# Moving the update of the sample states from the mixer to the gate and up tiles of the next stage

## Chip, cores, metric

One NeuronCore of a Trainium2 chip. The metric is the device time of one launch in microseconds (us), lower is better. A kernel is described by the median over its runs; one execution is profiled.

## What is computed

One inference step of a two-layer decoder trunk on 512 prompt rows and 8 sample rows (one new token for each of 8 sequences), all in fp32. Each layer has a SwiGLU FFN, a token mixer (a gated DeltaNet head group beside a sliding-window attention group) and a second SwiGLU FFN. Each of the three adds to the residual stream `x` through shift, scale and gate vectors ("modulation") that come from a conditioning vector. Cut to what the change touches, the DeltaNet step of a sample row, per head, with a state S of 128 x 128:

```python
# one token per sample row: the chunk has length 1
S      = S * jnp.exp(g)                     # decay
v_new  = beta * (v - k @ S)                 # what the state does not yet hold
o      = q @ S + (q . k) * v_new            # output, then gated RMSNorm
S_new  = S + outer(k, v_new)                # is an output of the function
```

The output `o` needs the old state and `v_new`, not `S_new`: the updated state is only stored (`new_dn_S_sample`, 8 sequences x 4 heads x 128 x 128 for each of 2 layers). Nothing later in the step reads it.

## The kernel before

Activations stand transposed, 128 features on the partitions and 512 + 8 columns, cut into a half of 256 and a half of 264. Matrix products are done in fp32 precision by splitting weights and activations into a high and a low part (`whi`/`wlo`, `hh`/`hl`): ScalarE rounds the high part, VectorE subtracts to get the low part, and TensorE does three products. Weight blocks arrive by DMA on SyncE's queue (SP) into four buffers (`raw`), and `Stream` splits them in pieces of 512 columns up to eight pieces ahead of their use.

Program order on every engine is fixed when the program is built. A planner (`Clock`, L40; `Fill`, L101) keeps modelled times of each engine, and during the long weight products it is asked at many points (`fill.step()`, L138) whether a piece of other work may be put in. Pieces are Python generators with a rank; the one of lowest rank that is ready by the model runs up to its next `yield`. A `yield` of tiles means "ready when those are written", of a function "ready when it returns true". `step` asks for a free PSUM bank, for ScalarE at most 2.4 us and VectorE at most 7.7 us behind TensorE in the model (L31, L145), and for nothing else.

An FFN (`ffn`, L849) has gate and up tiles f = 0 to 21 in two parts (0 to 10, 11 to 21), each part followed by a down projection. The first tiles (the `head`) are plain; from tile 3 a gate and up pair is done by `seven()` (L886) with seven block products where eight would be plain. It needs sums and differences of the weight blocks (`sum`, VectorE) and of the activations (`th`, made from `ht` by `combine`, L811, as the FFN starts), and its products of the two columns are put together by ScalarE (`u`) and VectorE (`g`, `u`). Its banks: `pa` and `pc` are the two halves of an `acc` buffer, `pb` an `aux` buffer into which five of the products accumulate with reads in between.

The mixer (`mix`, L1036) does the input projection, then attention and DeltaNet as filling work, then the output projection (`tail`, L770), whose tiles are added to `x` by VectorE (`xupdate`, L689). The sample part of DeltaNet is `dn_sample` (L1389), with `sample_pair` (L1417) for each pair of heads: it takes 7 slots (`hold(7)`), loads four state tiles `st` of 128 x 512 (four sequences of one head each), does the products with them, stores the rows of `v_new` to DRAM (`vnd`), loads them back spread over all partitions (`bv`), decays the states on GpSimd (L1486), adds the outer products on VectorE, four per state tile (L1496), and stores the tile (L1498). After that the second pair begins. In the trace the state tiles are called `s`, and the helper lines stand for all operations: L322 DMA, L328 matrix products, L338 transposes, L355 ScalarE, L363 VectorE, L374 and L376 GpSimd.

Most tiles share 51 slots of SBUF. `used` counts the named ones, `given` those taken by `hold` until they are given back; `given` is set to 0 as a mixer starts (L1039), and four that are held for the first output weights (`open_keep`, L1800) stay in the count until the next mixer. The modulation vectors are made by `ada_gen` (L515) at rank 9 from 18 groups per layer, each of eight loads (`ada`, 256 KB) and eight narrow products; a group is loaded when `fits()` (L525) finds room: 51 slots less `spares`, which is 13 during the gate and up tiles and 4 in the down projections (L982, L984). Layer 1's 18 groups are done in layer 0's second FFN.

Of the kernel before, what the change touches and what calls it, by code (L numbers as in the profile page):

```python
# [12 lines left out]
ALU = mybir.AluOpType  # L13
# [4 lines left out]
KD = D // 128  # L18
# [7 lines left out]
SLOTS = 51  # L26
# [276 lines left out]
class Ops:  # L303
# [68 lines left out]
    def pool(self, f, **k):  # L372
        if f == "memset":
            self.nc.gpsimd.memset(k["out"], k["value"])  # L374
        else:
            getattr(self.nc.gpsimd, f)(**k)  # L376
        self.clk.run("pool", 0.1 + 0.003 * self.cols(k["out"]), [k["out"]], self.aps(k, ("in_", "in0", "in1")))

    def tt(self, **k):
        self._dve("tensor_tensor", self.cols(k["out"]), k)  # L380

    def stt(self, **k):
        self._dve("scalar_tensor_tensor", self.cols(k["out"]), k)
# [22 lines left out]
def trunk(ctx, tc, xT, cT, cst, rope, vec, gu1, dn1, win, wba, wout, gu2, dn2, ada,  # L406
# [12 lines left out]
    mm, act, tt, stt, ts, dma, pool = ops.mm, ops.act, ops.tt, ops.stt, ops.ts, ops.dma, ops.pool  # L419
    fill = Fill(clk)  # L420

    used, given = set(), [0]
# [52 lines left out]
    def ada_load(l, g):  # L475

        t = []
        for k in range(KD):
            a = slot("ada", F32, (128, 512))
            dma(out=a, in_=ada[l, g, k])  # L480
            t.append(a)
        ada_live.extend(t)
        return t
# [26 lines left out]
    room = [True]  # L510

    spares = [13]
    mod_done = {(0, 0), (0, 1)}

    def ada_gen(l0):  # L515

        todo = []

        def more():
            if not todo and room[0] and mods and mods[0][0] <= l0:  # L520
                l, j = mods.pop(0)
                todo.extend((l, j, u) for u in range(2))
            return todo

        def fits():  # L525
            return len(used) + KD <= SLOTS - spares[0]

        queue, pa = [], None
        while True:
            while more() and len(queue) < 2 and fits():  # L530
                l, j, u = todo.pop(0)
                queue.append((l, j, u, ada_load(l, 2 * j + u)))
            if not queue:
                if not more():
                    return
                yield fits
                continue
            l, j, u, t = queue.pop(0)
            yield t
            if not u:  # L540
                pa = aux()
            ada_mm(t, pa, u)
            if u:
                m_sb = ada_out(pa)
                yield m_sb,
                ada_turn(l, 2 * j, m_sb, None, 2)
                drop(m_sb)
                mod_done.add((l, j))
            else:
                yield ()  # L550
# [298 lines left out]
    def ffn(l, j, norm, nxt, last, first=None, plain=3):  # L849
# [7 lines left out]
        def go(n=1):  # L857
            for _ in range(min(n, len(late))):
                late.pop(0)()
# [26 lines left out]
        def seven():  # L886

            pa, pb, pc = banks.pop(0) if banks else (None, aux(), None)  # L890
            if pa is None:
                u = acc()
                pa, pc = u[:, 0], u[:, 1]
            if pb is None:
                pb, pc = aux(), aux()
            t = slot("g")
            u1, u2 = (slot("u", F32, (128, 2, 264)) for _ in range(2))
            t0, t1 = t[:, 0:256], t[:, 256:520]

            def of_h(a, k0, n):  # L900
                return lambda _, part, k: hh[a][part][:, k0 + k, 0:n]

            def of_t(i, c, n=264):
                return lambda _, part, k: th[k][i + part][:, c, 0:n]

            def prod(bank, n, src, first):
                w = W.take()
                for k in range(4):
                    mmk(bank[:, 0:n], w, k, src, k, 0, first and k == 0, k == 3, join=not first)
                    W.advance(W.out - 1)  # L910
                    if k % 2:
                        fill.step()
                go()

            prod(pb, 264, of_h(0, 0, 264), True)
            act(out=u1[:, 0], in_=pb[:, 0:264], func=AF.Copy)
            prod(pa, 256, of_h(0, 4, 256), True)
            tt(out=t0, in0=pa[:, 0:256], in1=u1[:, 0, 0:256], op=ALU.add)
            prod(pb, 264, of_t(0, 1), False)
            act(out=u1[:, 1], in_=pb[:, 0:264], func=AF.Copy)  # L920
            act(out=t0, in_=t0, func=AF.Silu)
            prod(pc, 264, of_t(0, 0), True)
            act(out=u2[:, 1], in_=pc[:, 0:264], func=AF.Copy)
            prod(pb, 264, of_t(2, 0), False)
            tt(out=u2[:, 1], in0=pb[:, 0:264], in1=u2[:, 1], op=ALU.add)
            prod(pc, 264, of_h(1, 4, 264), False)
            tt(out=t1, in0=pc[:, 0:264], in1=u1[:, 1], op=ALU.add)
            prod(pb, 256, of_t(2, 1, 256), False)
            act(out=t1, in_=t1, func=AF.Silu)
            tt(out=t0, in0=t0, in1=pb[:, 0:256], op=ALU.mult)  # L930

            def end():
                tt(out=t1, in0=t1, in1=u2[:, 1], op=ALU.mult)
                drop(u1, u2)

            later(end, *split(t))
# [36 lines left out]
        for part, (f0, f1) in enumerate(PARTS):  # L973
            nk = f1 - f0
            for f in range(max(f0, 2), f1):
                if f < plain:
                    pg = product(h_src)
                    pu = product(h_src)
                    gate(pg, pu)
                    continue  # L980
                fill.until(lambda: len(th) == 4)
                spares[0] = 13  # L982
                seven()
            spares[0] = 4  # L984
            go(len(late))
            if part:
                room[0] = False
                for x_ in th:
                    drop(*x_)

            def g_src(a, p, k):
                o, n = HALF[a]
                return (ghi, glo)[p][f0 + k][:, o:o + n]

            fill.until(lambda: (l, 3 * j + 2) in mod_done)
            if part:
                if nxt:
                    ops.table(EXP)
                    n1 = (l, j + 1) if j < 2 else (l + 1, 0)
                    fill.until(lambda: {(n1[0], 3 * n1[1]), (n1[0], 3 * n1[1] + 1)} <= mod_done)  # L1000
                    nrm = nxt()
            for m in range(KD - 2 if part else KD):
                p = product(g_src, nk)
                for a in range(2):
                    xupdate(l, j, m, p[a], a)
                    if nrm is not None:
                        nrm.square(m, a)
                if part and last:
                    dma(out=y_o[:, m], in_=x[:, m])
            if part:  # L1010
                y, z = KD - 2, KD - 1
                items = [(0, y, True, True, True), (0, z, True, True, True), (1, y, False, False, True), (1, z, False, False, True)]
                tail(l, j, items, nk, nrm, g_src, last)
            drop(*ghi[f0:f1], *glo[f0:f1])
# [21 lines left out]
    def mix(l, norm):  # L1036
# [380 lines left out]
        def sample_pair(pr, qv, beg, d8, i8, bc, on):  # L1417

            hs = slice(2 * pr, 2 * pr + 2)
            st = [slot("s0", F32, (128, 4, 128), True) for _ in range(4)]  # L1420
# [54 lines left out]
            bv = []  # L1475

            def load(i):
                bv.append(slot("bv", F32, (128, 4, 128), True))
                o = 32 * (i // 2) + 4 * (i % 2)
                dma(out=bv[i], in_=rows[o:o + 4].partition_broadcast(128))  # L1480

            load(0)
            load(1)
            for i in range(4):
                h, s1 = 2 * pr + i // 2, 4 * (i % 2)
                pool("tensor_tensor", out=st[i], in0=st[i],  # L1486
                     in1=bc[:, h, s1:s1 + 4].unsqueeze(2).to_broadcast([128, 4, 128]), op=ALU.mult)
            yield vr,
            p = aux((128, 2, 32))
            ops.transpose(p.rearrange("p h s -> p (h s)"), vr[:, 2], cs[P, C_ID:C_ID + 64])  # L1490
            stt(out=on[:, hs], in0=p[:, :, 0:NS], scalar=V[:, V_DNW:V_DNW + 1], in1=zs[:, hs], op0=ALU.mult, op1=ALU.mult)
            for i in range(4):
                yield bv[i], st[i]
                h, s1 = 2 * pr + i // 2, 4 * (i % 2)
                for c in range(4):
                    stt(out=st[i][:, c], in0=bv[i][:, c], scalar=qv[:, h, 1, s1 + c:s1 + c + 1], in1=st[i][:, c],  # L1496
                        op0=ALU.mult, op1=ALU.add)
                dma(out=ss_o[l, :, 16 * pr + 4 * i:16 * pr + 4 * i + 4, :], in_=st[i])  # L1498
                if i < 2:
                    load(i + 2)  # L1500
            given[0] -= 7

        def out_sample(src, k0):
            hi, lo = hh[1]
# [575 lines left out]
```

## Time and profile before

| | |
|---|---|
| median of 3 runs | 2230.0 us (2226.77 to 2231.2) |
| the profiled execution | 2231.2 us, span 2229.4 us |
| mean granted TensorE clock | 0.984 of full speed |
| TensorE matmul / weight load busy | 96% / 90% |
| VectorE, ScalarE, GpSimd busy | 69%, 49%, 4% |
| HBM traffic | 287.76 MB, 129 GB/s |

Busy time is the time in which an engine works on an instruction; the span runs from the first instruction to the last. The stages of layer 0 lie at about 0 to 430 us (first FFN), 430 to 745 (mixer), 745 to 1180 (second FFN); those of layer 1 at 1180 to 1546, 1546 to 1845 and 1845 to 2229. In a timeline, a row gives the start, the time from the start of its first to the end of its last instruction, engine, line, operation, output and inputs, shapes, the count and in brackets the idle time of the engine before it with what ended it. Durations of neighbouring instructions overlap by some 0.08 us on VectorE and more on TensorE.

### The profile page before, as it was taken

The page shows a single profiled execution, that of the slowest core. Times are in us where ns is not written, and L with a number is a line of the kernel's source. Part 1 is how long each engine was busy: PE and PEld are TensorE (multiplying, and loading weights), DVE is VectorE, ACT ScalarE, POOL GpSimd, SP SyncE. Part 2 cuts the span into 40 slices and gives each one's busy share as a digit, 9 for nine tenths or more (in the row PEclk, how much of TensorE's full clock was granted, in tenths as well). Part 3 has the DMA queues.
Part 4 walks back from the last instruction along what each step waited for, and adds up shares of the span by engine and source line. Part 5 has one row for each costly group of instructions (what it writes and reads, how often), then busy time and mean ns, then how long its engine had stood idle before and what let it go on. Part 6 is the DMA issues. An engine that isn't in the chain of part 4 may idle for free.

```text
span 2229.4 us, 43763 instructions
## 1 busy us (share of the span) xinstructions
PE 2134.5 (96%) x17254; PEld 2015.0 (90%) x17254; DVE 1541.4 (69%) x3530; ACT 1091.0 (49%) x2342; POOL 80.5 (4%) x139
## 2 busy tenths in 40 slices
PE   7999999999978999999998999999999889999999
PEld 5898899998877889889998999999988779999999
DVE  5783596567767778458748947855686678865972
ACT  4462365356744445336535634644656345542651
POOL 0000000001011000000000000000010110000000
PEclk9999999999989999999999999999999899999999
DMA  8539634343223574773322332334332242333332
GB/s 287 198 123 305 225 105 145 105 89 103 68 70 105 192 249 139 272 261 107 103 95 69 106 106 91 105 98 106 94 102 64 71 137 86 98 104 93 107 108 72
DMA packets 177534, 287.76 MB, mean 129 GB/s; under 512 B 50448, under 2 KB 96176, under 8 KB 177328
## 3 DMA queue, kind: packets, MB, share of 16 engines
q1 hardware_dynamic: 177328, 284.96, 40.7%
q8 instruction: 135, 2.21, 0.4%
q14 instruction: 71, 0.58, 0.1%
HBM read 271.55 MB, written 14.41 MB: 128 GB/s over the span
## 4 chain that ended last, share of the span: by engine, by line
PE 83%; DVE 12%; ACT 3%; issue 1%; DMA 1%; SPq 0%; DVEq 0%; ACTq 0%
PE acc L328 48%; PE aux L328 34%; DVE wlo L363 2%; PE aux L338 1%; DVE s L363 1%; DVE cy L363 1%; DVE t L363 1%; DVE hl L363 1%; DVE y L363 1%; DVE sum L363 0%; DVE x L363 0%; ACT whi L355 0%; DVE w L363 0%; ACT s L355 0%; DMA bv<-vnd 0%
## 5 line engine op out<-in xcount | busy, mean ns | idle before, releaser
L355 ACT ACTIVATE whi<-raw 128x512 fp32r<-128x512 f32 (+1 forms) x597 | 361.5, 616 | 423.3 <-PE acc L328 359.7
L328 PE MATMUL acc<-hh,whi 128*128 128x256 f32 (+1 forms) x1640 | 421.6, 294 | 18.0 <-DVE x L363 9.2
L363 DVE TENSOR_TENSOR wlo<-raw,whi 128x512 fp32r<-128x512 f32 (+1 forms) x597 | 390.6, 672 | 47.5 <-ACT whi L355 46.5
L328 PE MATMUL acc<-hh,wlo 128*128 128x256 f32 (+1 forms) x1640 | 407.0, 285 | 12.0 <-DVE wlo L363 12.0
L328 PE MATMUL acc<-hl,whi 128*128 128x256 f32 (+1 forms) x1640 | 406.8, 285 | 1.6 <-DVE hl L363 1.4
L328 PE MATMUL aux<-th,whi 128*128 128x264 f32 (+1 forms) x1800 | 338.4, 285 | 2.5 <-ACT u L355 2.4
L328 PEld LDWEIGHTS acc<-hh,whi 128*128 128x128 f32 x1640 | 288.7, 191 | 42.7 <-issue 20.4
L328 PEld LDWEIGHTS acc<-hh,wlo 128*128 128x128 f32 x1640 | 288.5, 191 | 14.4 <-DVE wlo L363 14.4
L328 PEld LDWEIGHTS acc<-hl,whi 128*128 128x128 f32 x1640 | 288.2, 191 | 2.4 <-DVE hl L363 2.2
L328 PEld LDWEIGHTS aux<-th,whi 128*128 128x128 f32 x1800 | 278.5, 189 | 6.4 <-ACT u L355 2.9
L328 PE MATMUL acc<-ghi,whi 128*128 128x256 f32 (+1 forms) x1320 | 274.3, 284 | 2.7 <-DVE x L363 2.7
L328 PE MATMUL acc<-ghi,wlo 128*128 128x256 f32 (+1 forms) x1320 | 272.2, 282 | 0.0
L328 PE MATMUL acc<-glo,whi 128*128 128x256 f32 (+1 forms) x1320 | 271.8, 282 | 0.0
L328 PE MATMUL aux<-th,wlo 128*128 128x264 f32 (+1 forms) x900 | 255.4, 284 | 0.0
L363 DVE SCALAR_TENSOR_TENSOR x<-acc,mt,x 128x256 f32<-128x256 f32 x136 | 61.6, 480 | 265.2 <-PE acc L328 265.2
L355 ACT ACTIVATE whi<-sum 128x512 fp32r<-128x512 f32 x300 | 187.8, 628 | 75.6 <-PE acc L328 39.8
L328 PEld LDWEIGHTS acc<-ghi,whi 128*128 128x128 f32 x1320 | 206.9, 188 | 16.8 <-issue 16.8
L328 PEld LDWEIGHTS acc<-ghi,wlo 128*128 128x128 f32 x1320 | 207.0, 188 | 0.0
L328 PEld LDWEIGHTS acc<-glo,whi 128*128 128x128 f32 x1320 | 206.7, 188 | 0.0
L363 DVE TENSOR_TENSOR wlo<-sum,whi 128x512 fp32r<-128x512 f32 x300 | 199.8, 686 | 8.3 <-ACT whi L355 7.3
L328 PE MATMUL aux<-hh,whi 128*128 128x264 f32 x604 | 172.6, 286 | 0.0
L328 PE MATMUL aux<-hl,whi 128*128 128x264 f32 x604 | 171.9, 285 | 0.5 <-DVE hl L363 0.5
(326 smaller groups left out, 3628.8 us busy)
## 6 DMA issues: line engine op xcount, KB each, us to landing
raw<-in_gu SPq DMA_DIRECT2D x176, 512.0 KB, 3.6
ada<-in_ada SPq DMA_DIRECT2D x288, 256.0 KB, 5.6
raw<-in_dn SPq DMA_DIRECT2D x64, 512.0 KB, 3.6
raw<-in_win SPq DMA_DIRECT2D x44, 512.0 KB, 3.8
raw<-in_dn SPq DMA_DIRECT2D x64, 192.0 KB, 3.2
raw<-in_wout SPq DMA_DIRECT2D x22, 512.0 KB, 4.5
s<-in_s SPq DMA_DIRECT2D x16, 256.0 KB, 3.9
bv<-vnd SPq DMA_DIRECT2D x16, 256.0 KB, 3.9
```

The lines of the kernel that those rows point to most:

```text
L328: self.nc.tensor.matmul(out, lhsT=lhsT, rhs=rhs, start=start, stop=stop, skip_group_check=join)
L338: self.nc.tensor.transpose(out, in_, ident)
L355: self.nc.scalar.activation(**k)
L363: getattr(self.nc.vector, f)(**k)
```

## The change

The decay, the outer products and the store leave `sample_pair` for a generator of their own, `sample_state`, one for each pair, at rank 9.5. It waits before each state tile until `calm[0]` is true. `ffn` sets that after each `seven()` with f of 4 or more, and clears it when the gate and up tiles of the second part are done. The loads of `bv` go along, one before each update; the decay is done by VectorE (`tt`) in place of GpSimd. A pair gives back three slots as it ends and one for each updated state tile, and `fits()` of the modulation loads now counts the given slots too.

```diff
--- before.py
+++ after.py
@@ -510,6 +510,7 @@
     room = [True]
 
     spares = [13]
+    calm = [False]
     mod_done = {(0, 0), (0, 1)}
 
     def ada_gen(l0):
@@ -523,7 +524,7 @@
             return todo
 
         def fits():
-            return len(used) + KD <= SLOTS - spares[0]
+            return len(used) + given[0] + KD <= SLOTS - spares[0]
 
         queue, pa = [], None
         while True:
@@ -981,7 +982,10 @@
                 fill.until(lambda: len(th) == 4)
                 spares[0] = 13
                 seven()
+                calm[0] = f >= 4
             spares[0] = 4
+            if part:
+                calm[0] = False
             go(len(late))
             if part:
                 room[0] = False
@@ -1479,26 +1483,26 @@
                 o = 32 * (i // 2) + 4 * (i % 2)
                 dma(out=bv[i], in_=rows[o:o + 4].partition_broadcast(128))
 
-            load(0)
-            load(1)
-            for i in range(4):
-                h, s1 = 2 * pr + i // 2, 4 * (i % 2)
-                pool("tensor_tensor", out=st[i], in0=st[i],
-                     in1=bc[:, h, s1:s1 + 4].unsqueeze(2).to_broadcast([128, 4, 128]), op=ALU.mult)
             yield vr,
             p = aux((128, 2, 32))
             ops.transpose(p.rearrange("p h s -> p (h s)"), vr[:, 2], cs[P, C_ID:C_ID + 64])
             stt(out=on[:, hs], in0=p[:, :, 0:NS], scalar=V[:, V_DNW:V_DNW + 1], in1=zs[:, hs], op0=ALU.mult, op1=ALU.mult)
+
+            given[0] -= 3
+            fill.add(sample_state(pr, qv, bc, st, bv, load), 9.5)
+
+        def sample_state(pr, qv, bc, st, bv, load):
             for i in range(4):
+                yield lambda: calm[0]
+                load(i)
+                h, s1 = 2 * pr + i // 2, 4 * (i % 2)
+                tt(out=st[i], in0=st[i], in1=bc[:, h, s1:s1 + 4].unsqueeze(2).to_broadcast([128, 4, 128]), op=ALU.mult)
                 yield bv[i], st[i]
-                h, s1 = 2 * pr + i // 2, 4 * (i % 2)
                 for c in range(4):
                     stt(out=st[i][:, c], in0=bv[i][:, c], scalar=qv[:, h, 1, s1 + c:s1 + c + 1], in1=st[i][:, c],
                         op0=ALU.mult, op1=ALU.add)
                 dma(out=ss_o[l, :, 16 * pr + 4 * i:16 * pr + 4 * i + 4, :], in_=st[i])
-                if i < 2:
-                    load(i + 2)
-            given[0] -= 7
+                given[0] -= 1
 
         def out_sample(src, k0):
             hi, lo = hh[1]
```

## Rows read from the trace of the kernel before

**Rows 1.** The page, busy time, share of the span and instructions of each engine.

```profile
PE 2134.5 (96%) x17254; PEld 2015.0 (90%) x17254; DVE 1541.4 (69%) x3530; ACT 1091.0 (49%) x2342; POOL 80.5 (4%) x139
```

**Rows 2.** Windows: length, busy PE, PEld, DVE, ACT, POOL, then PEclk, DMA share, GB/s.

```profile
697.00:745.00 48.00, 42.21 (x364) 38.79 (x364) 34.69 (x107) 19.67 (x49) 4.58 (x13) 1.00 0.48 158
1796.10:1844.10 48.00, 42.34 (x365) 38.90 (x365) 34.77 (x107) 19.74 (x49) 4.58 (x13) 1.00 0.48 158
```

**Rows 3.** Chain that ended last, 660 to 745 us: start, us, what.

```profile
697.41 1.92 DVE s L363 x7
...
705.65 1.11 DVE s L363 x4
...
730.87 3.87 DMA bv<-vnd
```

**Rows 4.** Timeline of PE, 705 to 745 us, rows with a wait for `x`.

```profile
710.40 0.39 PE L328 MATMUL acc<-hh,whi 128*128 128x256 f32 x1 [1.23 <-DVE x L363]
...
724.52 0.38 PE L328 MATMUL acc<-hh,whi 128*128 128x256 f32 x1 [1.65 <-DVE x L363]
...
731.87 0.38 PE L328 MATMUL acc<-hh,whi 128*128 128x256 f32 x1 [1.02 <-DVE x L363]
...
738.61 0.36 PE L328 MATMUL acc<-hh,whi 128*128 128x256 f32 x1 [0.78 <-DVE x L363]
```

**Rows 5.** Windows of one gate and up tile and of down tiles, layer 1's first FFN.

```profile
1300.00:1350.00 50.00, 50.00 (x421) 50.00 (x420) 20.83 (x51) 11.48 (x19) 0.00 (x0) 1.00 0.32 101
1386.30:1396.45 10.15, 10.15 (x86) 10.15 (x85) 9.19 (x18) 6.36 (x15) 0.00 (x0) 1.00 0.36 106
```

**Rows 6.** Timeline of DVE and POOL, 696 to 726 us.

```profile
697.15 2.18 DVE L363 SCALAR_TENSOR_TENSOR s<-bv,misc,s 128x128 f32<-128x128 f32 x8
...
717.96 4.04 POOL L376 TENSOR_TENSOR s<-s,bc 128x512 f32<-128x512 f32 x4 [20.63 <-PE aux L328]
...
719.22 1.85 DVE L363 TENSOR_SCALAR vr<-vr,r 64x128 f32<-64x128 f32 x2
...
725.30 0.27 DVE L363 TENSOR_SCALAR vr<-vr,r 64x128 f32<-64x128 f32 x1
```

**Rows 7.** Whole run: a group of POOL (busy, mean ns), and DMA issues (KB, us to landing).

```profile
L376 POOL TENSOR_TENSOR s<-s,bc 128x512 f32<-128x512 f32 x16 | 16.2, 1046 | 69.2 <-PE aux L328 69.2
...
raw<-in_gu SPq DMA_DIRECT2D x176, 512.0 KB, 3.6
...
bv<-vnd SPq DMA_DIRECT2D x16, 256.0 KB, 3.9
```

**Rows 8.** Timeline of DVE and PE inside the same gate and up tile.

```profile
1389.96 0.69 DVE L363 TENSOR_TENSOR sum<-raw 128x512 f32<-128x512 f32 x1
1390.57 0.42 DVE L363 TENSOR_TENSOR g<-acc,u 128x256 f32<-128x256 f32 x1
...
1391.40 0.41 PE L328 MATMUL acc<-th,whi 128*128 128x264 f32 x2
...
1394.59 0.43 DVE L363 TENSOR_TENSOR u<-aux,u 128x264 f32<-128x264 f32 x1 [0.59 <-PE aux L328]
...
1395.76 0.40 PE L328 MATMUL aux<-th,whi 128*128 128x256 f32 x2
```

**Rows 9.** Timeline of DVE and PE, 1210 to 1220 us, and PE's window (busy, PEclk, DMA).

```profile
1210.71 1.32 DVE L363 TENSOR_TENSOR th<-y,th 128x528 fp32r<-128x528 f32 x2
...
1211.43 0.51 PE L328 MATMUL aux<-th,whi 128*128 128x264 f32 x2 [2.39 <-ACT u L355]
...
1214.83 0.81 PE L328 MATMUL acc<-th,whi 128*128 128x264 f32 x2 [0.69 <-DVE g L363]
...
1210.00:1220.00 10.00, 7.88 (x40) 0.66 0.36 105
```

**Rows 10.** A modulation group: its products in PE's timeline, its loads' landing in the page.

```profile
978.08 1.92 PE L328 MATMUL aux<-ada,sc 128*32 128x512 f32 x16
...
ada<-in_ada SPq DMA_DIRECT2D x288, 256.0 KB, 5.6
```

## The prediction

> **What bounds the kernel now.** The page's busy shares come first [rows 1]: TensorE 96%, VectorE 69%, ScalarE 49%, GpSimd 4%. TensorE sets the end, so a change is worth the TensorE idle time that it removes or makes, and both have to be read in the two stages it touches. The change leaves TensorE's own work as it is.
>
> First the mixer's end, from the transposition of the first pair's sample output to the last tile of the output projection: 48.00 us in each layer, with TensorE busy 42.21 and 42.34 [rows 2]. So 5.8 us a layer is all that this stretch can give. The chain of waits of that stretch [rows 3] shows the state update on it three times: seven outer products at 697.41, four at 705.65, and the load of the broadcast rows at 730.87. TensorE's own waits [rows 4] say where it ends up: four times (and four more in layer 1) an output product waits for VectorE's `x` update, 1.23 + 1.65 + 1.02 + 0.78 = 4.68 us. VectorE does its queue in order, and the `x` update stood behind state work.
>
> Then the gate and up tiles. One tile takes 10.15 us; TensorE is busy for all of it at full clock, and VectorE for 9.19 [rows 5]. Only 0.96 us of VectorE's time is free per tile. In the down tiles it is busy 20.83 of 50.00 us [rows 5], so 58% is free there.
>
> **The change, part by part.**
>
> *Removed from the mixer.* Per layer 32 outer products of 128x128 (back to back 2.18 us for eight [rows 6], less 0.08 us of drain: 0.26 us each, 8.4 us), eight decays of GpSimd (16 cost 16.2 us in the run [rows 7]), eight loads of broadcast rows, eight stores. What lies on the path, wait by wait [rows 4]: at 710.40 the four products before it (1.1 of the 1.23 us); at 731.87 the eight products before its `x` (1.02); at 738.61 four more products and the late load (0.78). At 724.52 the culprit is GpSimd: while its decays ran from 717.96 to 722.00, two small multiplications of `vr` took 1.85 us together; the same operation without GpSimd beside it took 0.27 us [rows 6]. Of that wait I take 1.3 us, the 1.85 less twice 0.27. Sum 1.1 + 1.0 + 0.8 + 1.3 = 4.2 us a layer, **8.4 us** in both. The eight products at 697 are on the chain, but TensorE then has transposes and the attention product to do, so I count nothing for them. Bounds: at most all idle time, 5.8 us a layer; at least minus 2 us, one wait of that size made by the new order, since the planner re-orders everything after the first pair and the second pair starts sooner.
>
> *Added to the gate and up tiles.* The same 32 products, and the decay as a VectorE operation. Before has no such decay; its price is bounded by GpSimd's 1.0 us [rows 7] and by VectorE's 512-column sums and subtractions, which start 0.61 us apart [rows 8]. It is the same form as the latter: 0.61. One state is 0.61 + 4 x 0.26 = 1.65 us, eight are **13.2 us of VectorE a layer**. They become eligible from tile 5 on (tiles count from 0; `calm` is set after tile 4), and nothing in `step` looks at the free VectorE time: it asks for less than 7.7 us of backlog and a ScalarE at most 2.4 us behind. Both pairs' generators then run in turn, each round bounded by a load (3.9 us to landing [rows 7]) and by VectorE's delay. With 3.3 us of VectorE work per round and four rounds I expect some 30 us, three tiles.
>
> What covers it? Three tiles give 3 x 0.96 = 2.9 us. The rest must make something late. In each tile TensorE waits on two hand-overs: VectorE's first `g` starts at 1390.57 and lasts 0.42, TensorE goes on in the other half of that bank at 1391.40, 0.4 us later; the `u` sum starts at 1394.59, lasts 0.43, and TensorE's last product accumulates onto the bank it reads at 1395.76, 0.7 us later [rows 8]. VectorE idles 0.59 us before the second, waiting for TensorE: that is most of the 0.96. State work that enters ahead of such a hand-over delays it one for one. Without relief TensorE loses 13.2 - 2.9 - 0.4 = 9.9 us a layer. Relief: the low parts of the weights are subtracted up to a tile ahead, and the planner puts off a split whose sum is over 1 us away, so two or three of the 0.61 us subtractions slip past a hand-over; I take 1.5 us off. **8.4 us a layer, 16.8 us in both.** Lower bound: all slips past, 0 us. Upper bound: nothing hidden, 13.2 us a layer, and a lowered clock on top.
>
> The trace has a precedent. In layer 1's first FFN the combination of `ht` into `th` leaves VectorE behind as the first such tile starts; TensorE waits 2.39 and 0.69 us in it, and in 10 us it does 40 matmuls at a granted clock of 0.66, between the 2.4 and 1.2 GHz levels [rows 9]; a steady tile does 86 in 10.15 us at 1.00 [rows 5]. 40 matmuls are worth 4.7 us: 5.3 of 10 us are lost.
>
> The Trainium skill has a rule that speaks against this move ("Perfetto Trace Analysis", Optimizing Scalar/DVE Operations): when VectorE is saturated, hand work off to ScalarE or GpSimd; here work goes from GpSimd to VectorE in the stage where VectorE is fullest. By that rule alone the time would rise. The same section warns that GpSimd and VectorE share a read port so that such a move may not help; the slowed `vr` multiplications agree.
>
> *DMA.* Sixteen transfers a layer leave SP's queue in the mixer and join it in the gate and up stage. A store there waits for its products with weight loads behind it; these are issued about a tile ahead of their sums and land in 3.6 us [rows 7], so a hold-up under some 5 us costs nothing. I cost it at zero; if VectorE falls further behind than that, a sum comes late and the same hand-overs pay.
>
> *Slots.* `fits` now counts `given`: after the mixer that is 4 for the kept weights and 8 for the states. With 16 `th` slots, 22 of gates, 4 and 8 for a group, a down stage needs 50 of its 47, where 46 fitted before. So most modulation loads of layer 1 move from layer 0's second FFN into its second half and into layer 1's first FFN. A group's products cost TensorE 1.92 us [rows 10] wherever they run. Moved, not added: zero. Bounds: minus 4 us (the waits of rows 9 filled by such a group) to plus 4 us (such a tile in the other FFN).
>
> **Sum.** The profiled execution took 2231.2 us for its 2229.4 us span: 2231.2 - 8.4 + 16.8 = 2239.6. It lies 1.2 us above the median of 2230.0; against that median 2238.4. I say **2238**.
>
> **Rivals.**
> *A, forecast:* the update crowds the hand-overs, 2233 to 2250. For: 0.96 us free per tile, no VectorE test in `step`. Chance 0.50.
> *B, the cover holds (faster):* lags stay short enough for the split-off subtractions to slip, or the ScalarE test spreads the states into the down tiles with their 58% of free VectorE. It decides at 0.96 / 1.65 = 0.6 states per tile entering ahead of hand-overs: at or below that the free time covers them. Cost at most 3 us in all, time 2230 - 8.4 + 3 = 2225 (2219 to 2226). For: `calm` stays on through the down stage of the first half. Against: generators re-arm at once. Chance 0.28.
> *C, nothing moves:* the waits for `x` go, but half of what A counts is paid, 2230 - 8.4 + 8.4 = 2230 (2226 to 2234). Chance 0.18.
> *D, the moved modulation loads make a stage wait* for its modulation: a modulation is two groups, and in series each takes a load's 5.6 us [rows 10] and 1.9 us of products; 15 us, over 2253. Nothing in the slot count calls for it. Chance 0.04.
>
> **Numbers.** 0.2% (4.5 us) is about what a measurement of this kernel can tell from no change. Faster 0.28 (B), within it 0.20 (C and the edge of A), slower 0.52 (A, D). The range 2222 to 2248 leaves out the best of B, the worst of A, and D; A's own is 2233 to 2250.
>
> **What would show it.** Right: in the mixer's last 48 us the waits for `x` shrink from 4.7 to under 1 us and the `vr` multiplications cost 0.27 us; in tiles 5 to 8 of the second FFNs tiles longer than 10.15 us, with TensorE waiting on `g` and `u` by 5 us or more a layer. Wrong: those tiles keep 10.15 us, or the `out_ss` stores are spread into the down stage; or the mixer's waits stay under other names.

## The result, and the profile after

The changed kernel takes 2240.56 us (median of four runs, 2235.99 to 2243.34) against 2228.39 us for the kernel before on the same chip (median of four): **slower by about half a per cent**, ratio 1.0055, 95% interval 1.0039 to 1.0072, or 12.2 us. The profiled execution of after took 2238.27 us for a span of 2236.2 us. TensorE's work did not grow. The page of after, busy time and share by engine (against [rows 1]):

```profile
PE 2133.4 (95%) x17254; PEld 2012.0 (90%) x17254; DVE 1548.2 (69%) x3546; ACT 1092.0 (49%) x2342; POOL 65.0 (3%) x123
```

The shares say nothing of the loss; the stages do. First the mixer's end. TensorE's waits for `x` in its timeline, after, 705 to 745 us (against [rows 4]):

```profile
715.46 0.39 PE L328 MATMUL acc<-hh,whi 128*128 128x256 f32 x1 [0.61 <-DVE x L363]
...
722.43 0.39 PE L328 MATMUL acc<-hh,whi 128*128 128x256 f32 x1 [0.58 <-DVE x L363]
...
729.05 0.36 PE L328 MATMUL acc<-hh,whi 128*128 128x256 f32 x1 [0.67 <-DVE x L363]
...
735.63 0.36 PE L328 MATMUL acc<-hh,whi 128*128 128x256 f32 x1 [0.67 <-DVE x L363]
```

Four waits of 4.68 us became four of 2.53 us, and the last comes 3.0 us earlier. The pair of `vr` multiplications takes 0.59 us in place of 1.85 [rows 6]; VectorE's timeline of after:

```profile
703.02 0.59 DVE L363 TENSOR_SCALAR vr<-vr,r 64x128 f32<-64x128 f32 x2
```

Then the gate and up tiles of layer 1's second FFN, one row for each of tiles 5 to 8: length, busy PE, PEld, DVE, ACT, POOL, then PEclk, DMA share, GB/s (against [rows 5]):

```profile
1919.40:1932.70 13.30, 10.60 (x86) 10.18 (x84) 13.03 (x29) 7.08 (x14) 0.00 (x0) 1.00 0.37 106
1932.70:1947.70 15.00, 11.99 (x84) 11.78 (x85) 14.76 (x34) 5.90 (x12) 0.00 (x0) 0.89 0.69 216
1947.70:1961.40 13.70, 11.93 (x86) 11.72 (x85) 12.75 (x30) 6.42 (x13) 0.00 (x0) 0.88 0.54 176
1961.40:1971.60 10.20, 10.20 (x87) 10.20 (x86) 9.19 (x17) 6.37 (x13) 0.00 (x0) 1.00 0.42 135
```

Three tiles hold all eight states. They last 42.0 us where three steady ones last 30.4, so 11.6 us are lost; VectorE is busy for 40.5 of the 42.0. By the rows TensorE is idle for 7.5 us of them and busy for 34.5, 4.1 more than in three steady tiles, with a lowered granted clock in two. In layer 0 the same three last 13.3, 14.8 and 12.2 us, 9.9 us lost. What TensorE waits for in 1885 to 1995 us of after (us in total, times, longest), and VectorE's timeline within the second tile:

```profile
PE acc L328 <- DVE g L363: 5.9, 4, 3.0
PE aux L328 <- DVE u L363: 2.0, 1, 2.0
```

```profile
1935.81 0.69 DVE L363 TENSOR_TENSOR wlo<-raw,whi 128x512 fp32r<-128x512 f32 x1
1936.41 1.14 DVE L363 SCALAR_TENSOR_TENSOR s<-bv,misc,s 128x128 f32<-128x128 f32 x4
1937.46 0.69 DVE L363 TENSOR_TENSOR s<-s,bc 128x512 f32<-128x512 f32 x1
1938.06 0.43 DVE L363 TENSOR_TENSOR g<-g,u 128x264 f32<-128x264 f32 x1
1938.40 0.69 DVE L363 TENSOR_TENSOR wlo<-raw,whi 128x512 fp32r<-128x512 f32 x1
1939.01 0.69 DVE L363 TENSOR_TENSOR sum<-raw 128x512 f32<-128x512 f32 x1
1939.61 1.14 DVE L363 SCALAR_TENSOR_TENSOR s<-bv,misc,s 128x128 f32<-128x128 f32 x4
1940.66 0.69 DVE L363 TENSOR_TENSOR s<-s,bc 128x512 f32<-128x512 f32 x1
1941.26 0.43 DVE L363 TENSOR_TENSOR g<-acc,u 128x256 f32<-128x256 f32 x1
```

No row carries an idle time in brackets: VectorE runs without a gap, four products of one state (1.05 us from start to start) and the decay of the next (0.60) stand as a block ahead of the next `g`, and TensorE waits for that.

**The ledger, by the places of the same tile in both traces.** (Position after minus position before; it is one profiled execution of each, 6.8 us apart by their spans, where the medians are 12.2 apart.) At the first full tile of layer 0's second FFN after is 7.6 us ahead. Of that, 3.0 are there at the mixer's last wait for `x`. The head of the FFN gives 2.6, because before's granted clock fell in it and after's did not. The remaining 2.0 are a modulation group that before has done by then and after has not. The three long tiles cost 9.9. By the last gate and up tile of layer 1's first FFN after is 2.3 us ahead, again with one group still to come, so the modulation groups, which now lie partly there, returned 4.6. That last group takes 2.4, layer 1's mixer gives 3.1 and the head of the next FFN 2.7 (again at full clock in after alone), 3.4 in sum, and the tiles cost 11.6 against before's steady ones: 5.9 behind, 6.8 at the end.

### The profile page after: what moved, and what is told of

The parts are those of the page before. It is cut to its first block, busy times and chain, and to the rows that moved or that the text cites. A ratio compares the mean times of both kernels' runs of the same rounds, so it can differ in the third digit from the quotient of the medians.

```text
span 2236.2 us, 43737 instructions
## 1 busy us (share of the span) xinstructions
PE 2133.4 (95%) x17254; PEld 2012.0 (90%) x17254; DVE 1548.2 (69%) x3546; ACT 1092.0 (49%) x2342; POOL 65.0 (3%) x123
## 3 DMA queue, kind: packets, MB, share of 16 engines
q8 instruction: 135, 2.21, 0.4%
## 4 chain that ended last, share of the span: by engine, by line
PE 83%; DVE 12%; ACT 3%; issue 1%; DMA 1%; SPq 0%; DVEq 0%; ACTq 0%
PE acc L328 48%; PE aux L328 34%; DVE wlo L363 2%; DVE s L363 1%; PE aux L338 1%; DVE cy L363 1%; DVE t L363 1%; DVE sum L363 1%; DVE y L363 1%; DVE hl L363 1%; DVE g L363 1%; ACT whi L355 0%; DVE x L363 0%; DVE w L363 0%; ACT s L355 0%
## 5 line engine op out<-in xcount | busy, mean ns | idle before, releaser
L363 DVE TENSOR_TENSOR wlo<-sum,whi 128x512 fp32r<-128x512 f32 x300 | 200.2, 685 | 10.2 <-ACT whi L355 8.1
```

The lines of the kernel that those rows point to most:

```text
L363: getattr(self.nc.vector, f)(**k)
```

## The experiments

Eleven kernels ran, one of them twice, in three groups, each timed against the kernel before on its own chip (2229.3, 2227.9 and 2227.8 us). "Off before" is the difference of the medians. The two theories: the overflow of VectorE work in the tiles is what costs (the forecast), or something that comes along with it (transfers, the count of slots, the clock).

**The gain alone.** The changed kernel without the update and with the old slot count; the updated sample states are not stored.

```diff
-            given[0] -= 3
-            fill.add(sample_state(pr, qv, bc, st, bv, load), 9.5)
+            given[0] -= 7
```

> Leaves the update of the sample states out altogether (their output isn't written); the modulation loads are counted as before, so they stay where they were. Theory (VectorE is overfull in three gate and up tiles, and the mixer only gains): this shows the gain alone, 6.4 us by the two traces, so about 2222; tiles stay 10.15 us. The prediction's step: 8.4 us, 2220. Rival (the waits for x come back under other names, and the whole loss is in the mixer or the moved loads): 2228 or more.

Measured 2219.29 us, ratio 0.9951 [0.9939, 0.9962]: 10.0 us off before (8.5 to 13.6 by the interval), where the prediction had 8.4. The change as a whole costs 12.2, so by the medians the update in the tiles costs 22.2. The waits for `x` are those of after, 2.5 us in layer 0. The mixer's end accounts for some 3.0 us in each layer (in layer 1, from the last tile of the first FFN to the first full tile of the second, 445.1 us in place of 448.1). In layer 0 this kernel is 8.0 us ahead of before at its first full tile, and 5.3 us at the last wait for `x` (733.33 in place of 738.61). What goes beyond the 3.0 lies in two stretches in which TensorE's clock differs. Windows of the middle of that mixer and of that head, in the kernel before and then in this one (columns as above):

```profile
640.00:660.00 20.00, 15.52 (x85) 14.69 (x86) 9.01 (x17) 4.40 (x11) 6.48 (x5) 0.66 0.24 59
770.00:780.00 10.00, 7.04 (x44) 6.84 (x43) 9.02 (x25) 5.59 (x10) 1.96 (x8) 0.74 1.02 365
780.00:790.00 10.00, 10.00 (x78) 10.00 (x78) 9.69 (x22) 5.81 (x11) 0.00 (x0) 0.91 0.21 80
```

```profile
640.00:660.00 20.00, 14.76 (x103) 14.04 (x104) 10.77 (x22) 5.45 (x14) 6.47 (x5) 0.83 0.25 60
760.00:770.00 10.00, 7.51 (x62) 7.24 (x61) 7.00 (x21) 5.65 (x11) 1.96 (x8) 1.00 0.91 313
770.00:780.00 10.00, 9.54 (x79) 9.54 (x80) 9.51 (x24) 4.83 (x9) 0.00 (x0) 1.00 0.69 254
```

In the head both wait about 3 us for the first `wlo`. After it, before's granted clock fell to a mean of 0.74 and then 0.91 over these stretches, this kernel's and after's stayed at 1.00. In layer 1 this kernel falls to 0.66 at that place too. The instructions don't decide it: up to the tiles of layer 0's second FFN all kernels made from the changed one issue the same instructions on TensorE, VectorE and ScalarE. Yet that head lasts 38.7 us in seven of their traces, at a clock of 1.00, and 41.3 in three others, where the clock falls. Layer 0's mixer likewise lasts 288.9 to 289.2 us in eight traces and 291.4 to 291.9 in three (after is one of these). What does decide it isn't settled here.

So some 6 of the 10.0 us are what the ends of the two mixers gave. The five runs of this kernel had a mean granted clock of 0.986 to 0.988, the eleven of before 0.982 to 0.985; that the change brings the difference, and with it the other 4 us, is not shown.

**The transfers alone.** The changed kernel with loads, stores and generators in the tiles, without the decay, and with one product of two columns in place of four of 128.

```diff
-                tt(out=st[i], in0=st[i], in1=bc[:, h, s1:s1 + 4].unsqueeze(2).to_broadcast([128, 4, 128]), op=ALU.mult)
-                for c in range(4):
-                    stt(out=st[i][:, c], in0=bv[i][:, c], ...
+                stt(out=st[i][:, 0, 0:2], in0=bv[i][:, 0, 0:2], ...
```

> The changed kernel with the loads of bv, the generators, the waits and the stores where they are, but without the decay, and with one product of 2 columns in place of the four of 128 per state (so the states stored aren't updated). Theory (VectorE's time): tiles 5 to 7 fall back to 10.15 us, some 21 us less than the changed kernel, about 2219. Rival (the stores and loads on SP's queue delay the weights): the tiles stay 12 to 15 us, 2236 to 2241.

2220.79 us, 0.995 [0.9938, 0.9962]; tiles of 10.13 to 10.58 us, in both layers together 0.8 us more than steady ones. So the transfers cost next to nothing in the tiles: 8.5 us off before, where the kernel without the update (and with the old slot count) has 10.0. The changed kernel has the same transfers and the same count and lies 12.2 behind before, so VectorE's work costs 20.7 us.

**The same work in the down projection.** The changed kernel with `calm` true only during the first part's down projection.

```diff
-                calm[0] = f >= 4
...
-            if part:
-                calm[0] = False
+            calm[0] = not part
...
             drop(*ghi[f0:f1], *glo[f0:f1])
+            calm[0] = False
         return nrm
```

> The changed kernel with the update allowed only in the down projection of the first part of each FFN (where VectorE is busy 42% of the time), not beside gate and up tiles. Theory: TensorE's hand-overs have 58% of free VectorE around them, so the update costs under 1 us a layer, and the 6.4 us of the mixer stay: 2215 to 2222, faster than both kernels. Rival (transfers on SP's queue): down tiles grow, 2232 or more.

2218.79 us, 0.995 [0.9937, 0.9963]: the whole update is there, and the time is that of the kernel without it (which has the old slot count). A second time, in another group:

> The changed kernel with the states let in by the down projection of part 0 alone, a second time, beside the kernel with the old slot count: ratio 0.995 again, 10 to 11 us under the kernel before. Rival: the first time was favourable, 0.997 or more.

2216.71 us, 0.9954 [0.9942, 0.9967], 11.1 us off before. All tiles take 10.13 us. This version beats both kernels.

**The slot count**, undone in the changed kernel and in the one that updates in the down projection (one edit, two kernels):

```diff
-            return len(used) + given[0] + KD <= SLOTS - spares[0]
+            return len(used) + KD <= SLOTS - spares[0]
```

> The changed kernel, but the modulation loads don't count the given slots, so layer 1's groups stay in layer 0's second FFN as before. Theory: tiles 5 to 7 of both second FFNs stay long; what the moved groups gave back (about 6.7 us by the traces, most of it the waits in layer 1's first FFN) is lost again, 2240 to 2246. Rival (the moved loads are what makes the changed kernel slower): 2228 to 2234.

2244.02 us, 1.0061 [1.0046, 1.0076]: 14.7 behind before where after is 12.2. The intervals overlap, so beside the update in the tiles what the count is worth can't be told from nothing.

> The changed kernel with the states let in by the down projection of part 0 alone, and the slots that are held not counted for the modulation loads, so that those stay in layer 0's second FFN as before. Moved groups cost or give nothing: the same as with the new count, ratio 0.995. Rival: the new count gave the 3 to 4 us that the changed kernel lost without it, ratio 0.9965.

2236.18 us, 1.0039 [1.0027, 1.0052]: 19.5 us over the same kernel with the new count, far outside either expectation. Windows of the down projection, layer 0, first with the new count and then with the old one (columns as above):

```profile
900.00:950.00 50.00, 50.00 (x419) 50.00 (x418) 29.04 (x73) 11.59 (x19) 0.00 (x0) 1.00 0.48 149
```

```profile
900.00:950.00 50.00, 43.58 (x311) 33.68 (x310) 22.60 (x61) 7.62 (x14) 0.00 (x0) 0.97 0.64 205
```

TensorE does 311 matrix products in place of 419, and VectorE is not the limit (22.6 of 50 us). With the old count, what SP's queue waited for in 900 to 960 us (us in total, times, longest), part of its timeline, and TensorE's wait in the same window:

```profile
SPq L322 <- PE aux L328: 18.7, 6, 6.9
SPq L322 <- DVE s L363: 6.9, 4, 3.5
SPq L322 <- DMA ada<-in_ada: 5.7, 6, 2.4
```

```profile
914.03 1.53 SPq L322 DMA_DIRECT2D bv<-vnd  x2
915.62 0.90 SPq L322 DMA_DIRECT2D raw<-in_dn  x2
916.62 11.29 SPq L322 DMA_DIRECT2D ada<-in_ada  x8
927.96 0.42 SPq L322 DMA_DIRECT2D out_ss<-s  x1
```

```profile
PE aux L328 <- DMA ada<-in_ada: 8.1, 4, 2.9
```

In this trace SP issues in the order of the program. Eight modulation loads took 11.3 us to issue, because SP stood before `aux` products that had yet to be done; stores, broadcast rows and weights queued behind, and TensorE got its modulation data late. In the kernel without the update and with the old count SP waits only 8.1 us on those products (890 to 960 us), and the stage is full of TensorE work (50.00 of 50.00 us). So the new count is what lets the down projection hide the update. From the last tile of the first part to the first of the second the trace with the old count takes 103.3 us, with the new one 73.5. Six modulation groups in that stretch explain 11.5 of the 29.8 us by [rows 10]; the other 18, an estimate, are nearly all of the 19.5.

**How many states a tile can hide.** A count of admissions in place of a flag: one state for each tile from tile 5 on, the last two in the down projection; and in a second kernel two (`2 * int(f >= 4)`).

```diff
-                calm[0] = f >= 4
+                calm[0] = int(f >= 4)
...
+            calm[0] = 0 if part else 8
...
                 yield lambda: calm[0]
+                calm[0] -= 1
```

> The changed kernel with one state tile allowed in each of the gate and up tiles 5 to 10, the last two in the down projection behind them. Theory: 1.65 us against 0.96 free, 0.7 us lost in each of six tiles, less the 0.4 us hand-over slack: some 7.5 us more than down_only (2218.8), 2225 to 2228. Rival 1 (the weight subtractions slip and absorb it): 2218 to 2221. Rival 2 (state work in a gate and up tile is paid in full whatever its pace): 2235 or more.

2221.59 us, 0.9967 [0.9954, 0.998]; tiles of 10.70 us (10.51 for the first). That is less than expected, 4.2 to 4.8 us over the update in the down projection by the differences to before.

> The changed kernel with two states let in by each gate and up tile from tile 5 on (so four tiles take all eight). Overflow of VectorE work: a tile with one state hid 1.1 of its 1.65 us, so one with two is 3.3 - 1.1 = 2.2 us longer, 12.3 us, eight such tiles in both layers 17.6 us over the kernel without the update, ratio about 1.003. Rival 1, dense clusters and the lowered clock are what costs: with waits under 2 us the granted clock stays at 1.00, tiles under 11.3 us, ratio 0.999 or less. Rival 2, any crowding costs what the full crowding costs: ratio 1.0055 as in the changed kernel.

2232.82 us, 1.0024 [1.0013, 1.0036]; tiles of 12.34 us (12.1 for the first), four in each layer, as expected. One tile without a state (from the kernel without the update), with one, with two, all in layer 1 (columns as above):

```profile
1933.01:1943.14 10.13, 10.13 (x87) 10.13 (x85) 9.19 (x17) 6.36 (x13) 0.00 (x0) 1.00 0.34 104
```

```profile
1930.00:1940.70 10.70, 10.47 (x87) 10.26 (x86) 10.67 (x23) 6.55 (x14) 0.00 (x0) 1.00 0.47 147
```

```profile
1930.00:1942.34 12.34, 10.67 (x84) 10.25 (x84) 12.30 (x28) 6.51 (x13) 0.00 (x0) 1.00 0.53 172
```

The third row's tile is longer by 2.21 us for 3.30 us of work, the second's by 0.57 for 1.65: either hides 1.1 us, about the idle time of a steady tile (0.94), and the rest is paid one for one. TensorE's clock stays at 1.00 in both, so the loss does not need the lowered clock.

**More work of the same kind**: the decay done twice on each state in the changed kernel.

```diff
                 tt(out=st[i], in0=st[i], in1=bc[:, h, s1:s1 + 4].unsqueeze(2).to_broadcast([128, 4, 128]), op=ALU.mult)
+                tt(out=st[i], in0=st[i], in1=bc[:, h, s1:s1 + 4].unsqueeze(2).to_broadcast([128, 4, 128]), op=ALU.mult)
```

> The changed kernel with each decay done twice on VectorE (so the states stored are wrong by one decay): 8 x 0.61 = 4.9 us more of VectorE a layer in the same tiles. Theory (VectorE is full there, so more work is paid one for one, less the free 0.96 us of a further tile): 8 to 10 us more than the changed kernel, 2248 to 2251. Rival (the cost is the transfers, or a fixed price of each piece): 2239 to 2243.

2253.53 us, 1.0113 [1.0098, 1.0127], 13.5 us above after (by the differences to before) for 16 x 0.60 = 9.6 us of added work. The tiles of layer 1 take 16.21, 18.56 and 13.79 us, and the three of both layers are 14.8 us longer than in after: dearer than one for one by the traces, while the intervals of the medians would allow one for one.

**The decay back on GpSimd**, still beside the tiles in the program:

```diff
-                tt(out=st[i], in0=st[i], ...
+                pool("tensor_tensor", out=st[i], in0=st[i], ...
```

> The changed kernel with the decay on GpSimd, as before, in the same tiles. Theory: 4.9 us of VectorE a layer less there, 2230 to 2232. Rival (a GpSimd decay beside VectorE holds VectorE up as it did the small vr multiplications, 1 us each, so nothing is saved): 2238 to 2242.

2236.43 us, 1.0039 [1.0025, 1.0052], between the two expectations. It is 3.6 us less than after by the two differences to before (their intervals overlap), though the long tiles of layer 1 shrank by 6.0 us (12.57, 12.24 and 11.16) and those of layer 0 by 4.2. GpSimd's timeline shows where the rest went:

```profile
766.62 1.97 POOL L376 TENSOR_TENSOR ht<-hs,mt 128x8 f32<-128x8 f32 x8 [60.93 <-DMA ada<-in_ada]
768.55 9.80 POOL L376 TENSOR_TENSOR s<-s,bc 128x512 f32<-128x512 f32 x8
```

GpSimd had nothing ahead of the decays in its queue and ran all eight in the head of the FFN, over 50 us ahead of the tiles they were written beside: `calm` orders the program, it doesn't hold an idle engine. There VectorE prepares the first operands. Groups of VectorE from 768 to 779 us (count, busy us, mean ns), and TensorE's wait from 755 to 815 us (us in total, times, longest), in this kernel:

```profile
L363 DVE SCALAR_TENSOR_TENSOR hl<-ht,mt,hh 128x256 fp32r<-128x256 f32 x6 | 6.0, 998 | 0.2 <-ACT hh L355 0.2
```

```profile
PE acc L328 <- DVE wlo L363: 6.9, 1, 6.9
```

And after:

```profile
L363 DVE SCALAR_TENSOR_TENSOR hl<-ht,mt,hh 128x256 fp32r<-128x256 f32 x8 | 3.9, 482 | 0.4 <-ACT hh L355 0.4
```

```profile
PE acc L328 <- DVE wlo L363: 3.0, 1, 3.0
```

Beside GpSimd the same operation takes 998 ns instead of 482, and TensorE's wait grows by 3.9 us. The head lasts 45.1 us in place of 38.7; beside the longer wait its granted clock fell (0.52 in 770 to 780 us, where after has 1.00). At the first full tile this kernel is 4.8 us behind after.

**The prediction's terms for the mixer**, each in the kernel before. Its decay left out:

```diff
-                pool("tensor_tensor", out=st[i], in0=st[i],
-                     in1=bc[:, h, s1:s1 + 4].unsqueeze(2).to_broadcast([128, 4, 128]), op=ALU.mult)
```

> The kernel before without the decay on GpSimd (the states stored aren't decayed), the products and transfers left in the mixer. The prediction's term for the slowed vr multiplications: 1.3 us a layer, 2226 to 2227. Rival (the output product waits for x anyway): 2229.

2226.41 us, 0.999 [0.9981, 0.9999]: 1.5 us off before, not 2.6. The `vr` pair takes 0.59 us, the wait after it falls from 1.65 to 1.03 us. And its products cut down:

```diff
-                for c in range(4):
-                    stt(out=st[i][:, c], in0=bv[i][:, c], ...
+                stt(out=st[i][:, 0, 0:2], in0=bv[i][:, 0, 0:2], ...
```

> The kernel before, with the four outer products of each state tile cut to one product of two columns (so the stored sample states are wrong: 32 products a layer become 8 tiny ones); decays, loads and stores stay in the mixer. The prediction's terms for the products, 1.1 + 1.0 + 0.8 us a layer, say 5.8 us off the kernel before: a ratio of 0.9974, tiles of the output projection waiting for x about 1.3 + 0.5 us a layer instead of 4.7. Rival: the x waits go but other work takes their place, 0 to 2 us off, ratio 0.999 or more.

2222.29 us, 0.9976 [0.9967, 0.9985]: 5.5 us off before, 5.8 expected. But the waits for `x` in layer 0 fell only from 4.7 to 3.3 us, not to 1.8. So the time agrees with the expectation and the waits do not: in both layers together they give some 2.6 of the 5.5 us, and where the rest comes from is not shown.

## Why the prediction was right, and where its terms were off

The sign, the mechanism of the tiles and the time (2238 forecast, 2240.56 measured) came out. By the medians both large terms were too small, the gain by 1.6 us and the loss by 5.4 (3.9 against the kernel with the transfers alone), and their errors partly cancel: that the time came within 3 us is luck in part. By the traces the mixer's term was too large.

*The mixer, 8.4 us forecast, 10.0 measured by the medians, some 6 to be seen in the mixers of the traces.* The step "1.1 + 1.0 + 0.8 + 1.3" took each wait for `x` as nearly all state work. Every one of them keeps 0.58 to 0.67 us in after, and the sum is the same 2.5 us without any update; the `x` update itself takes 0.48 us in VectorE's timeline, most of such a wait. The waits gave 2.0 to 2.15 us a layer, half of the term, and "from 4.7 to under 1 us" in the list of signs was wrong. The 1.3 us for GpSimd's decays came to 0.75 a layer, the interval of that run reaching from 0.1 to 2.1. The mixer's end came 3.0 us earlier a layer all the same, 6 in both in place of 8.4. The rest of the 10.0 lies, in the traces, where the clock differs (1.00 in place of 0.74 and 0.91 in the head of layer 0's second FFN). No term of the sum stands for that, and as the same instructions ran at either clock, it is not shown to come from the change.

*The tiles, 16.8 us forecast, 22.2 measured (20.7 against the kernel with the transfers alone).* The count held: 0.60 for a decay (0.61 taken from VectorE's subtractions), 0.26 for a product, eight states in three tiles from tile 5 on, TensorE waiting on `g` and `u`. What failed is "Relief: ... I take 1.5 us off", and in layer 1 the full use of the 2.9 + 0.4 us that I let the tiles hide. Of 13.2 us a layer 11.6 were lost in layer 1 and 9.9 in layer 0, so 1.6 and 3.3 us were hidden in three tiles, where paced states hide 1.1 in each. Layer 0 comes out as the forecast without relief; layer 1 lies 1.7 above it. The lowered clock stood in the upper bound, and it came: 0.89 and 0.88 in layer 1's second and third tile, 0.88 in layer 0's second. It can't be the main cause, since VectorE is busy for 14.76 of 15.00 us in the second tile and TensorE would wait for it at any clock. In the third, VectorE idles 0.95 us of 13.70, and there the slow clock may cost something; that is argued, not shown. (In layer 0 the third tile kept a clock of 1.00 and took 12.2 us, VectorE being busy for all of it, 1.5 less than in layer 1.) The tiles lost 21.5 us by the trace, which lies between the 22.2 and the 20.7 of the medians.

*Transfers at zero*: right in the tiles (with the transfers alone they are 0.8 us longer in both layers together). *Moved modulation loads at zero, within 4 us*: 2.5 us in the changed kernel, by medians whose intervals overlap, 4.6 in the ledger. But the same count is worth 19.5 us once the update lies in the down projection. I had treated the slots as an edit apart; they decide whether the free VectorE time of the down stage can be used at all.

*The rivals.* B's mechanism, states spread until free time covers them, did not happen in the changed kernel. Its limit of 0.6 states per tile fits what was measured (nothing ran below it): one state per tile overflows by 0.57 us, and 0.96 + 0.4 us of cover in the forecast stand against 1.1 measured. Its other half, the down projection with 58% of VectorE free, is the version that wins. C asked for half the loss and D for a wait on modulation in a stage; after shows neither (its only listed wait for `ada`, 6.8 us at the start of the run, is 6.6 in before).

*The rule of the Trainium skill that was weighed*, "Perfetto Trace Analysis" in Optimizing Scalar/DVE Operations, says that handing work from a full VectorE to GpSimd may not help, as the two share a port. The decay back on GpSimd shows both sides: the tiles lost 10.2 us of their length, and VectorE's operations beside it went from 482 to 998 ns.

## What to carry to other kernels

Price filler by the stage that it lands in: on an engine that is 91% busy in the stage, a piece hides what is idle in that tile and no more, however low the engine's share over the whole run. Pace such work by what one tile can hide or move it to a stage with room, and check that the slots and the in-order queue of that stage are free, too. Of a wait that you mean to remove, take off first what the awaited operation itself needs.

## What the runs showed of the hardware that was not expected

- Eight GpSimd multiplications of 128x512 slowed VectorE's operations of 128x256 to 2.07 times their time (998 against 482 ns), and took 1.2 us each themselves, where 16 in the mixer took 1.05 [rows 7].
- An instruction placed late in the program on an idle engine ran as soon as its inputs were there, over 50 us ahead of the work it was written beside.
- Beside waits of 2 to 3 us the granted clock was 0.88 to 0.89 in three of the six long tiles of after and 1.00 in the other three; with the same work paced, waits of at most 0.9 us in those tiles, it stayed at 1.00.
- One and the same stream of instructions took two lengths: the head of layer 0's second FFN, with its 3 us wait, 38.7 us at a clock of 1.00 or 41.3 us where the clock fell. Two traces can so differ by 2.7 us in such a place without any difference of the kernels. The four runs of after, too, lie at 2236 and 2238 us with a mean clock of 0.985 and 0.986, and at 2243 us (twice) with 0.980.
